# First chunk as two plain units, aligned accumulators, and a third pair of seven products in an fp32 encoder layer

## The chip, the cores and the metric

The kernel runs on one core of a Trainium2 chip. The metric is device time in microseconds (us) of one execution. The kernel before takes 2221.93 us (median of 3 runs, 2221.05 to 2222.04).

## What is computed

One encoder layer on 256 tokens of width 2048, in fp32. The change touches the two feed-forward halves:

```python
h = h + 0.5 * swiglu(rmsnorm(h, ffn1_norm[i]), ffn1_w_gate[i], ffn1_w_up[i], ffn1_w_down[i])
...  # mixer: neighbourhood attention, latent attention, gates, w_out
h = h + 0.5 * swiglu(rmsnorm(h, ffn2_norm[i]), ffn2_w_gate[i], ffn2_w_up[i], ffn2_w_down[i])
...  # per-layer embedding, final norm

def swiglu(x, w_gate, w_up, w_down):
    return (jax.nn.silu(x @ w_gate) * (x @ w_up)) @ w_down
```

The hidden width is 5632, that is 11 chunks of 512 columns; the inner width 2048 is 16 K tiles of 128.

## The kernel before

**Three matmuls for one.** Every operand is split into a rounded part hi and a rest lo (`split`, L89: ScalarE casts hi, VectorE subtracts to get lo). A product is then `triple` (L93): lo of x times hi of w, hi times hi, hi times lo, each a matmul of 128 columns of x against 128x512 of w.

**Joint blocks.** A `Block` (L170) computes gate and up of one chunk together, over 8 pairs of K tiles. Two token halves, two K tiles and two outputs make eight products per pair; a *plain pair* (`Plain`) does these eight, 24 matmuls. A *product pair* does seven products of sums (21 matmuls): its granule A (`SevenA`) holds three weights and forms sums of weights in place (L238, L240, L241 on VectorE), its granule B (`SevenB`) holds the four sums. `SEVEN` (L22) names the pairs that do so: 3 and 5. I write P0, P1, P2, A3, B3, P4, A5, B5, P6, P7 for a block's ten granules. The sums of x that go with them are the *forms*, made once per feed-forward half (`new_forms`, for the first pair `first_form`) and kept in X0 to X7.

**Accumulators.** The seven sums q1 to q7 of a block have fixed banks of PSUM (L192): q1 in bank 0, q6 in 1, q7 in 2, q3 in 3, q2, q4, q5 in 4 to 6; bank 7 is for transposes. A block's `early` evacuates q1, q6, q7, its `late` gives `first` (q2, q4) and `rest` (q5, q3, sigmoid, product). The result is transposed in two steps T0 and T1 (four small transposes each into bank 7, read by L310 on ScalarE and L311 on VectorE).

**Down.** After 4, 4 and 3 chunks (`PARTS`) four *units* of the down product follow. A unit takes two accumulators from banks 0 to 3 in turn (`acc_bank`, a counter that runs through the whole kernel). The mixer has one unit with a single accumulator, so the counter stands at an odd place when the second feed-forward half begins.

**What sets the order.** A list of granules, `grans`, is worked off at the end of the program: each step emits the matmuls of its granule, then the small tasks due at that step (`tasks`, filled by `at`). `convert` loads and splits granules ahead; a granule takes two of the six buffers W0 to W5 (an ordinary unit's granule one of W0 to W3), which come free when an earlier granule's matmuls are done. So at most three granules are split ahead. Raw weights come through three buffers R0 to R2 by DMAs from SP's queue. Each engine executes its own instructions in the order in which the program emits them. The last granule of a block, P7, calls `more[0]` (first), `convert`, `more[1]` (rest):

```python
        if ends:
            more[0]()
            convert()
            more[1]()
        free.extend(e.tags)
        for fn in tasks.pop(g, []):
            fn()
```

Of the kernel before, what the change touches and what calls it, by code (L numbers as in the profile page):

```python
# [14 lines left out]
P = 128  # L15
# [5 lines left out]
PARTS = ((0, 4), (4, 8), (8, 11))  # L21
SEVEN = {3, 5}  # L22
MLA_SCALE = 192 ** -0.5
# [4 lines left out]
def encoder_kernel(ctx, tc, x, p, ffn1_norm, ffn1_w_gate, ffn1_w_up, ffn1_w_down, mix_norm, w_in,  # L28
# [28 lines left out]

    seven_on = [True]
    spare = [7, 0, 1, 2]
    turn = {"acc": 0, "side": 0, "raw": 0}  # L60
# [4 lines left out]
    def bank():  # L65
        if seven_on[0]:
            turn["side"] += 1
            return psum_tile(spare[turn["side"] % len(spare)])
        turn["side"] += 1
        return psum_tile(4 + turn["side"] % 4)  # L70
# [29 lines left out]
    class Unit:  # L100
        def __init__(self, src, K, N, xop, evac, by_token=False, wide=False):
            self.src, self.K, self.N, self.xop, self.evac, self.by_token = src, K, N, xop, evac, by_token
            self.per = 4 if wide else 1024 // N
            self.load = 4 if wide else (2 * self.per if N == 512 else self.per)
            self.raw = self.ps = None
            self.kept = []
            for k0 in range(0, K, self.per):
                grans.append(Granule(self, k0, min(self.per, K - k0), wide))

    class Granule:  # L110
# [7 lines left out]
        def conv(self):  # L118
            u, k0, nk = self.u, self.k0, self.nk
            if k0 % u.load == 0:  # L120
                n = min(u.load, u.K - k0)
                u.raw = raw_piece([P, n, u.N])
# [47 lines left out]
    class Block:  # L170
        def __init__(self, srcs, form, early, late):
            self.srcs, self.form, self.early, self.late = srcs, form, early, late
            self.first = not grans
            self.q = {}
# [33 lines left out]
    class Plain(Pair):  # L208
        def conv(self):
            raw = first_raw(self) or raw_piece([P, 4, 512])  # L210
            self.blk.load(self.i, raw)
            self.hilo(4)
            if self.blk.first and self.i == 0:
                between = first_form()
                split(self.hi[:, 0:2, :], self.lo[:, 0:2, :], raw[:, 0:2, :])
                between()
                split(self.hi[:, 2:4, :], self.lo[:, 2:4, :], raw[:, 2:4, :])
                return
            split(self.hi, self.lo, raw)
# [11 lines left out]
    class SevenA(Pair):  # L231
        def conv(self):
            raw = first_raw(self) or raw_piece([P, 4, 512])
            raws[id(self.blk), self.i] = raw
# [8 lines left out]
        def matmuls(self):  # L243
            b, hi, lo = self.blk, self.hi, self.lo
            seven_on[0] = True
            f = b.form(self.i)
            for n, w, x in ((1, 0, 0), (2, 1, 1), (3, 2, 5)):
                b.add(n, f(x), hi[:, w, :], lo[:, w, :], n == 1 and self.i == max(SEVEN))

    class SevenB(Pair):  # L250
# [14 lines left out]
    def first_raw(p):  # L265
        return piece(f"H{p.i}", [P, 4, 512]) if p.blk.first and p.i < 4 else None

# [68 lines left out]
    forms = {}  # L336

    def new_forms(n, gname, js=(0, 1)):
        for j in js:
            i = 2 * n + j  # L340
            ps = bank()
            for k in range(2):
                for t in range(2):
                    PE.transpose(ps[:, k * T + t * P:k * T + t * P + P],
                                 h[:, t, (2 * i + k) * P:(2 * i + k + 1) * P], ident)
            z = piece("Z", [P, 8, P])
            gc = gcol[gname] + 2 * i
# [3 lines left out]
            S.activation(o1, p4[:, 0], AF.Copy, scale=gT[:, gc:gc + 1])
            S.activation(z[:, 2:4, :], p4[:, 1], AF.Copy, scale=gT[:, gc + 1:gc + 2])

            def minus(o, a, b):
                V.tensor_tensor(out=z[:, o, :], in0=z[:, a, :], in1=z[:, b, :], op=ALU.subtract)
            if seven:
                minus(4, 0, 3)
                minus(7, 1, 0)
                minus(5, 4, 1)
                V.tensor_tensor(out=z[:, 6, :], in0=z[:, 2, :], in1=z[:, 5, :], op=ALU.add)  # L360
                r, m = z[:, 1:8, :], 7
            else:
                V.tensor_tensor(out=z[:, 4:6, :], in0=z[:, 0:3:2, :], in1=z[:, 1:4:2, :], op=ALU.subtract)
                r, m = z[:, 0:6, :], 6
            f = piece(f"X{i}", [P, 2, m, P], F32R)
            split(f[:, 0], f[:, 1], r)
            forms[i] = f

    def first_form():
        ps = bank()  # L370
        for k in range(2):
            for t in range(2):
                PE.transpose(ps[:, k * T + t * P:k * T + t * P + P], h[:, t, k * P:(k + 1) * P], ident)
        f = piece("X0", [P, 2, 6, P], F32R)
        forms[0] = f
        p4 = ps.rearrange("p (k t c) -> p k t c", k=2, t=2)
        for k in range(2):
            S.activation(f[:, 0, 2 * k:2 * k + 2], p4[:, k], AF.Copy, scale=gT[:, k:k + 1])
        for k in range(2):
            V.scalar_tensor_tensor(out=f[:, 1, 2 * k:2 * k + 2], in0=p4[:, k], scalar=gT[:, k:k + 1],  # L380
                                   in1=f[:, 0, 2 * k:2 * k + 2].bitcast(F32), op0=ALU.mult, op1=ALU.subtract)

        def rest():
            z = piece("Z", [P, 8, P])
            for k in range(2):
                S.activation(z[:, 2 * k:2 * k + 2, :], p4[:, k], AF.Copy, scale=gT[:, k:k + 1])
            V.tensor_tensor(out=z[:, 4:6, :], in0=z[:, 0:3:2, :], in1=z[:, 1:4:2, :], op=ALU.subtract)
            split(f[:, 0, 4:6], f[:, 1, 4:6], z[:, 4:6, :])
        return rest

# [69 lines left out]
    def ffn(phase, wg, wu, wd, nxt):  # L460
# [43 lines left out]
        def down_evac(n, final):  # L504
# [545 lines left out]
    step[0] = -1  # L1050
    for a, b in ((256, 512), (512, 1024), (1024, 2048)):
        convert()
        nc.sync.dma_start(h[:, :, a:b], xr[:, :, a:b])
        if a == 256:
            new_forms(0, "ffn1", (1,))

    def begin(i):
        return lambda: new_forms(i // 2, "ffn1", (i % 2,))

# [6 lines left out]
    for i in range(2, 8):  # L1066
        tasks.setdefault((0, 1, 2, 2, 3, 4)[i - 2], []).append(begin(i))
    for n in range(4):
        tasks.setdefault(5 + n, []).append(late_stat(n))
    tasks.setdefault(30, []).append(lambda: gains(16, 72))  # L1070

    for g, e in enumerate(grans):
        step[0] = g
        if g == 3:
            del spare[1:]
        ends = isinstance(e, Pair) and e.end and not isinstance(e, SevenB)
        if g > 2 and not ends:
            convert()
        seven_on[0] = isinstance(e, Pair)
        more = e.matmuls()  # L1080
        if ends:
            more[0]()
            convert()
            more[1]()
        free.extend(e.tags)
        for fn in tasks.pop(g, []):
            fn()
        if g <= 2:
            convert()
    assert not tasks, sorted(tasks)  # L1090

# [38 lines left out]
```

## Time and profile before

| | |
|---|---|
| median of three runs | 2221.93 us |
| the profiled execution | 2220.76 us, of which span 2219.0 us |
| PE (TensorE) busy | 2186.1 us, 99% of the span |
| VectorE busy | 1471.8 us, 66% |
| ScalarE busy | 1030.8 us, 46% |
| mean granted TensorE clock | 0.993 |

TensorE works nearly all the time, so time goes in three ways only: matmuls that are issued, matmuls at the lower clock, and the few stretches in which TensorE waits. The shares of VectorE and ScalarE are means over stages; in the joint blocks they are higher.

### The profile page before, as it was taken

To read this page: it belongs to the slowest core of one execution; us is meant where nothing else is said; L and a number is where in the kernel's file an instruction comes from. 1 tells how busy PE (TensorE), PEld (TensorE's weight loads), DVE (VectorE), ACT (ScalarE), POOL (GpSimd) and SP (SyncE) were. 2 spreads that over 40 slices of the span, in tenths; PEclk is the share of its full clock that TensorE was granted. 3 is DMA by queue.
4 is the path that set the end of the run, shared out by engine and by line. 5 is a ranking of instruction groups with operands and counts; after the bars stand their busy time and mean duration, and the time that the engine had idled before them with its cause. 6 is when DMAs were issued, how large, how long until landed. Compare 5 with 4: busy or idle time off the path is not lost. (4 is left out here: it accounts for less than half of the span.)

```text
span 2219.0 us, 24699 instructions
## 1 busy us (share of the span) xinstructions
PE 2186.1 (99%) x9832; PEld 1801.9 (81%) x9832; DVE 1471.8 (66%) x1486; ACT 1030.8 (46%) x1042; POOL 35.8 (2%) x39
## 2 busy tenths in 40 slices
PE   8999999999999999999999999999999999999997
PEld 6788888888888887788888888887888878887886
DVE  6887468865786565555655556888558875687665
ACT  5544344543444454445544445545334543444453
POOL 0000000000000000040000000000000000000000
PEclk8999999999999999999999999999999999999999
DMA  5655555566556554475455555556555655566553
GB/s 193 218 190 198 194 195 179 190 215 198 175 192 207 162 183 139 135 213 182 146 192 191 191 184 199 171 188 212 188 171 195 213 192 191 180 204 210 178 174 126
DMA packets 211795, 413.54 MB, mean 186 GB/s; under 512 B 11704, under 2 KB 12288, under 8 KB 211552
## 3 DMA queue, kind: packets, MB, share of 16 engines
q1 hardware_dynamic: 210432, 408.46, 55.3%
q0 software_dynamic: 1216, 3.50, 0.7%
q8 instruction: 77, 1.26, 0.2%
q14 instruction: 38, 0.31, 0.0%
q10 hardware_dynamic: 32, 0.01, 0.0%
HBM read 409.83 MB, written 2.10 MB: 186 GB/s over the span
## 5 line engine op out<-in xcount | busy, mean ns | idle before, releaser
L91 DVE TENSOR_TENSOR W<-R,W 128x1024 fp32r<-128x1024 f32 (+2 forms) x587 | 965.7, 1660 | 500.3 <-ACT W L90 489.8
L90 ACT CAST W<-R 128x1024 fp32r<-128x1024 f32 (+2 forms) x587 | 816.2, 1402 | 796.2 <-PE B L96 367.4
L95 PE MATMUL B<-W,X 128*128 128x512 f32 x2132 | 842.8, 395 | 2.8 <-ACT W L90 1.5
L97 PE MATMUL B<-W,X 128*128 128x512 f32 x2132 | 833.1, 391 | 2.5 <-DVE W L91 2.4
L96 PE MATMUL B<-W,X 128*128 128x512 f32 x2132 | 832.1, 390 | 0.0
L97 PEld LDWEIGHTS B<-W,X 128*128 128x128 f32 x2132 | 401.3, 188 | 88.9 <-DVE W L91 4.2
L95 PEld LDWEIGHTS B<-W,X 128*128 128x128 f32 x2132 | 401.7, 188 | 87.8 <-issue 2.5
L96 PEld LDWEIGHTS B<-W,X 128*128 128x128 f32 x2132 | 401.7, 188 | 81.2
L95 PE MATMUL B<-W,H 128*128 128x512 f32 x832 | 327.4, 393 | 7.9 <-DVE pt L486 7.9
L97 PE MATMUL B<-W,H 128*128 128x512 f32 x832 | 325.3, 391 | 0.0
L96 PE MATMUL B<-W,H 128*128 128x512 f32 x832 | 325.2, 391 | 0.0
L95 PEld LDWEIGHTS B<-W,H 128*128 128x128 f32 x832 | 157.0, 189 | 41.1 <-ACT W L90 5.5
L97 PEld LDWEIGHTS B<-W,H 128*128 128x128 f32 x832 | 157.0, 189 | 33.0
L96 PEld LDWEIGHTS B<-W,H 128*128 128x128 f32 x832 | 157.1, 189 | 31.8
L310 ACT CAST H<-B 128x512 fp32r<-128x512 f32 x52 | 30.1, 587 | 183.3 <-PE B L327 183.3
L311 DVE TENSOR_TENSOR H<-B,H 128x512 fp32r<-128x512 f32 x52 | 35.6, 690 | 73.4 <-ACT H L310 73.4
L238 DVE TENSOR_TENSOR R<-R 128x1024 f32<-128x1024 f32 x43 | 52.7, 1225 | 1.5
L508 DVE SCALAR_TENSOR_TENSOR h<-B,h 128x512 f32<-128x512 f32 x48 | 32.9, 691 | 23.7 <-PE B L97 23.7
L315 ACT ACTIVATE X<-B,gT 128x256 fp32r<-128x256 f32 x40 | 15.7, 475 | 35.4 <-PE B L327 35.4
L240 DVE TENSOR_TENSOR R<-R 128x512 f32<-128x512 f32 x43 | 29.8, 692 | 1.5
L241 DVE TENSOR_TENSOR R<-R 128x512 f32<-128x512 f32 x43 | 29.8, 692 | 1.5
L327 PE MATMUL B<-ident,t 128*128 128x128 f32 x136 | 27.8, 272 | 0.0
(215 smaller groups left out, 942.4 us busy)
## 6 DMA issues: line engine op xcount, KB each, us to landing
R<-in_ffn_w_down_dram SPq DMA_DIRECT2D x88, 1024.0 KB, 5.1
R<-in_ffn_w_gate_dram SPq DMA_DIRECT2D x172, 512.0 KB, 3.7
R<-in_ffn_w_up_dram SPq DMA_DIRECT2D x172, 512.0 KB, 4.7
R<-in_w_in_dram SPq DMA_DIRECT2D x64, 1024.0 KB, 5.2
R<-in_w_out_dram SPq DMA_DIRECT2D x16, 1024.0 KB, 5.1
R<-in_w_pl_gate_dram SPq DMA_DIRECT2D x16, 1024.0 KB, 5.1
R<-in_w_branch_a_dram SPq DMA_DIRECT2D x8, 1024.0 KB, 5.1
R<-in_w_branch_b_dram SPq DMA_DIRECT2D x8, 1024.0 KB, 5.0
```

The source lines that it names most:

```text
L90: S.copy(hi, r)
L91: V.tensor_tensor(out=lo, in0=r, in1=hi.bitcast(F32), op=ALU.subtract)
L95: PE.matmul(o, xl, hi, start=start, stop=False)
L96: PE.matmul(o, xh, hi, start=False, stop=False)
L97: PE.matmul(o, xh, lo, start=False, stop=stop)
L238: V.tensor_tensor(out=raw[:, 0:4:3, :], in0=raw[:, 0:3:2, :], in1=raw[:, 3:4, :].to_broadcast([P, 2, 512]), op=ALU.add)
L240: V.tensor_tensor(out=raw[:, 2, :], in0=raw[:, 0, :], in1=raw[:, 2, :], op=ALU.add)
L241: V.tensor_tensor(out=raw[:, 1, :], in0=raw[:, 2, :], in1=raw[:, 1, :], op=ALU.add)
L310: S.copy(hi, ps.rearrange("p (k t) -> p k t", k=2))
L311: V.tensor_tensor(out=lo, in0=ps.rearrange("p (k t) -> p k t", k=2), in1=hi.bitcast(F32), op=ALU.subtract)
L327: PE.transpose(ps[:, k * T + t * P:k * T + t * P + P], srcs[t][:, (2 * j + k) * P:(2 * j + k + 1) * P], ident)
L508: V.scalar_tensor_tensor(out=hs, in0=ps[t], scalar=0.5, in1=hs, op0=ALU.mult, op1=ALU.add)
```

## The change

Four things change. (1) The first chunk of the first half is no joint block but two ordinary units, gate and then up, of 16 K tiles each, in granules of two K tiles; its forms of sums are made later (`more_forms`), while the up unit runs, and x is loaded in smaller pieces. (2) The accumulator counter is set to 0 at the first down unit of each part (`align`). (3) The product pairs are 2, 4 and 6, so a block is P0, P1, A2, B2, P3, A4, B4, P5, A6, B6, P7. (4) Since B6 stands right before P7, the tasks due at P7 (`early`) are emitted ahead of `first`.

```diff
-SEVEN = {3, 5}
+SEVEN = {2, 4, 6}
...
     class Unit:
-        def __init__(self, src, K, N, xop, evac, by_token=False, wide=False):
+        def __init__(self, src, K, N, xop, evac, by_token=False, wide=False, align=False):
+            self.align = align
...
+            self.early = not grans
+            if self.early:
+                self.load = 2
...
             if k0 == 0:
+                if u.align:
+                    turn["acc"] = 0
                 u.ps = [acc_bank() for _ in range(2 if u.N == 512 else 1)]
...
+    def first_forms(i):
+        p2 = plain_tiles(i)
...
+        for k in range(2):
+            S.activation(hi[k], p2[:, k], AF.Copy, scale=gT[:, 2 * i + k:2 * i + k + 1])
         for k in range(2):
+            V.scalar_tensor_tensor(out=lo[k], in0=p2[:, k], scalar=gT[:, 2 * i + k:2 * i + k + 1],
+                                   in1=hi[k].bitcast(F32), op0=ALU.mult, op1=ALU.subtract)
+
+        def keep():
+            z = zs[i // 4][:, i % 4].rearrange("p (k a) b -> p k (a b)", k=2)
             for k in range(2):
+                S.activation(z[:, k], p2[:, k], AF.Copy, scale=gT[:, 2 * i + k:2 * i + k + 1])
+        return keep
+
+    def more_forms(i):
+        e = tmp.tile([P, 4, P], F32, tag="s", name=nm("e"))
+        m = sums(zs[i // 4][:, i % 4], e, i)
+        split(forms[i][:, 0, 4:4 + m], forms[i][:, 1, 4:4 + m], e[:, 0:m, :])
...
+        def gate_evac(ps):
...
+        def up_evac(ps):
+            r = rstd[phase]
+            a = hold.pop("a")
+            for t in range(2):
+                V.scalar_tensor_tensor(out=a[t], in0=ps[t], scalar=r[:, t:t + 1], in1=a[t],
+                                       op0=ALU.mult, op1=ALU.mult)
...
+            at(1, tr(0))
+            at(2, tr(1))
+
         for c0, c1 in PARTS:
             for c in range(c0, c1):
-                block(c)
+                if grans:
+                    block(c)
+                else:
+                    unit(rows(wg, 0), 16, 512, first_xop, gate_evac)
+                    unit(rows(wu, 0), 16, 512, first_xop, up_evac)
...
                 unit(rows(wd[c0 * 512:c1 * 512], n * 512), 4 * (c1 - c0), 512, hop,
-                     down_evac(n, c1 == NC_FF), wide=True)
+                     down_evac(n, c1 == NC_FF), wide=True, align=(n == 0))
...
     for i in range(2, 8):
-        tasks.setdefault((0, 1, 2, 2, 3, 4)[i - 2], []).append(begin(i))
+        tasks.setdefault(i - 2, []).append(lambda i=i: first_forms(i)())
     for n in range(4):
-        tasks.setdefault(5 + n, []).append(late_stat(n))
-    tasks.setdefault(30, []).append(lambda: gains(16, 72))
+        tasks.setdefault(3 + n, []).append(late_stat(n))
+    for i in range(8):
+        tasks.setdefault(8 + i, []).append(lambda i=i: more_forms(i))
+    tasks.setdefault(7, []).append(lambda: gains(16, 72))
...
         if ends:
+            for fn in tasks.pop(g, []):
+                fn()
             more[0]()
```

VectorE's order where the up unit of the first chunk ends and the first joint block begins, in the changed kernel (W_81 is lo of P0's weights, W_86 of P1's, W_91 of A2's; e is a sum of x, X a form; B_67 and B_68 are the up unit's accumulators):

```order
L89 TENSOR_TENSOR W_81_520<-R_79_516,W_80_519 128x2048
L340 TENSOR_TENSOR e_535<-H_23_246 128x128 x2
...
L89 TENSOR_TENSOR X_27_275<-e_554,X_27_275 128x256
L89 TENSOR_TENSOR W_86_562<-R_84_558,W_85_561 128x2048
L340 TENSOR_TENSOR e_577<-H_23_246 128x128 x2
L340 TENSOR_TENSOR e_577<-e_577,H_23_246 128x128
L347 TENSOR_TENSOR e_577<-H_23_246,e_577 128x128
L89 TENSOR_TENSOR X_35_309<-e_577,X_35_309 128x512
L540 SCALAR_TENSOR_TENSOR t_417<-B_67_431,sm_388,t_417 128x512
L540 SCALAR_TENSOR_TENSOR t_418<-B_68_432,sm_388,t_418 128x512
```

The two L540 read the up unit's accumulators, banks 2 and 3. They stand behind the splits of P0 and P1 and the forms of pairs 4, 5 and 6.

VectorE's order between two joint blocks of a part, before (from the last evacuation of the old block: L91 are splits of P2 and A3, L238 to L241 the sums of weights, L311 reads T0):

```order
L490 SCALAR_TENSOR_TENSOR t_2222<-t_2222,sm_502,s_2253 128x512
L91 TENSOR_TENSOR W_329_2276<-R_327_2272,W_328_2275 128x2048
L91 TENSOR_TENSOR W_336_2311<-R_334_2307,W_335_2310 128x1536
L238 TENSOR_TENSOR R_334_2307<-R_334_2307 128x2x512
L240 TENSOR_TENSOR R_334_2307<-R_334_2307 128x512
L241 TENSOR_TENSOR R_334_2307<-R_334_2307 128x512
L311 TENSOR_TENSOR H_337_2341<-B_338_2342,H_337_2341 128x512
```

and in the changed kernel (the same place; L502 is L490, L240 to L243 are L238 to L241, L310 is L311):

```order
L502 SCALAR_TENSOR_TENSOR t_1194<-t_1194,sm_388,s_1192 128x512
L89 TENSOR_TENSOR W_183_1222<-R_181_1218,W_182_1221 128x1536
L240 TENSOR_TENSOR R_181_1218<-R_181_1218 128x2x512
L242 TENSOR_TENSOR R_181_1218<-R_181_1218 128x512
L243 TENSOR_TENSOR R_181_1218<-R_181_1218 128x512
L89 TENSOR_TENSOR W_189_1257<-R_181_1218,W_188_1256 128x2x512
L89 TENSOR_TENSOR W_189_1257<-R_181_1218,W_188_1256 128x1024
L310 TENSOR_TENSOR H_190_1286<-B_191_1287,H_190_1286 128x512
```

The split of P2 is gone from in front of the read of T0, and both splits of B2 now stand there.

TensorE's order at that place in the changed kernel (the last transpose of T0, the nine matmuls of A2, the first transpose of T1):

```order
L326 MATMUL B_339_2399<-ident,t_2306 128x128
L93 MATMUL B_343_2413<-W_330_2333,X_16_189 128x512
L94 MATMUL B_343_2413<-W_330_2333,X_16_189 128x512
L95 MATMUL B_343_2413<-W_331_2334,X_16_189 128x512
L93 MATMUL B_332_2340<-W_330_2333,X_16_189 128x512
L94 MATMUL B_332_2340<-W_330_2333,X_16_189 128x512
L95 MATMUL B_332_2340<-W_331_2334,X_16_189 128x512
L93 MATMUL B_335_2361<-W_330_2333,X_16_189 128x512
L94 MATMUL B_335_2361<-W_330_2333,X_16_189 128x512
L95 MATMUL B_335_2361<-W_331_2334,X_16_189 128x512
L326 MATMUL B_344_2423<-ident,pt_2307 128x128
```

In the kernel before the 24 matmuls of P2 stand between T0 and T1.

## Rows read from the trace of the kernel before

**Rows 1.** What TensorE waited for: us in total, times, longest us

```profile
PE B L95 <- DVE pt L486: 7.9, 3, 3.2
```

**Rows 2.** Timeline of TensorE: start us, us, engine, line, operation, [idle before <-releaser]

```profile
59.44 0.39 PE L95 MATMUL B<-W,X 128*128 128x512 f32 x1
...
68.28 0.45 PE L95 MATMUL B<-W,X 128*128 128x512 f32 x1
...
80.46 0.27 PE L327 MATMUL B<-ident,pt 128*128 128x128 f32 x1
```

**Rows 3.** A steady joint block: us, busy of PE, PEld, DVE, ACT, POOL

```profile
107.69:150.85 43.16, 43.16 (x196) 35.71 (x195) 35.42 (x32) 21.21 (x17) 0.00 (x0) 1.00 0.58 196
```

**Rows 4.** Groups by line and shape: busy us, mean ns | idle before

```profile
L90 ACT CAST W<-R 128x2048 fp32r<-128x2048 f32 x217 | 415.0, 1912 | 366.1 <-PE B L96 274.4 <-DMA R<-in_ffn_w_up_dram 35.7 <-DVE W L91 32.2
L90 ACT CAST W<-R 128x1024 fp32r<-128x1024 f32 x327 | 340.9, 1053 | 358.9 <-PE B L97 237.4 <-DVE R L238 86.1 <-PE B L96 22.4
...
L91 DVE TENSOR_TENSOR W<-R,W 128x2048 fp32r<-128x2048 f32 x217 | 494.9, 2290 | 265.5 <-ACT W L90 256.1 <-PE B L96 9.3
L91 DVE TENSOR_TENSOR W<-R,W 128x1024 fp32r<-128x1024 f32 x327 | 398.5, 1229 | 223.1 <-ACT W L90 222.0
L91 DVE TENSOR_TENSOR W<-R,W 128x1536 fp32r<-128x1536 f32 x43 | 75.3, 1752 | 11.7 <-ACT W L90 11.7
L238 DVE TENSOR_TENSOR R<-R 128x1024 f32<-128x1024 f32 x43 | 52.7, 1225 | 1.5
...
L240 DVE TENSOR_TENSOR R<-R 128x512 f32<-128x512 f32 x43 | 29.8, 692 | 1.5
```

**Rows 5.** Timeline of VectorE, steady block: start of `early`, last of `rest`

```profile
107.69 0.68 DVE L470 TENSOR_TENSOR pt<-B,t 128x512 f32<-128x512 f32 x1
...
110.18 0.69 DVE L479 TENSOR_TENSOR pt<-B,t 128x512 f32<-128x512 f32 x1 [0.48 <-PE B L97]
...
117.20 0.75 DVE L490 SCALAR_TENSOR_TENSOR t<-t,sm,s 128x512 f32<-128x512 f32 x1
```

**Rows 6.** Timeline of TensorE, first down units of the second half

```profile
1553.63 0.47 PE L95 MATMUL B<-W,H 128*128 128x512 f32 x1 [2.35 <-DVE pt L486]
...
1557.29 0.46 PE L95 MATMUL B<-W,H 128*128 128x512 f32 x1
...
2037.27 0.47 PE L95 MATMUL B<-W,H 128*128 128x512 f32 x1 [3.17 <-DVE pt L486]
...
2038.73 0.63 PE L95 MATMUL B<-W,H 128*128 128x512 f32 x1
...
2042.13 0.40 PE L97 MATMUL B<-W,H 128*128 128x512 f32 x1
```

**Rows 7.** Timeline of TensorE, first chunk

```profile
35.97 1.12 PE L344 MATMUL B<-ident,h 128*128 128x128 f32 x4 [3.00 <-ACT Z L352]
```

**Rows 8.** Timeline of ScalarE, first chunk: x, weights, squares

```profile
5.80 0.84 ACT L378 ACTIVATE X<-B,gT 128x256 fp32r<-128x256 f32 x2 [3.51 <-PE B L373]
...
16.11 1.91 ACT L90 CAST W<-H 128x2048 fp32r<-128x2048 f32 x1 [1.30 <-DMA H<-in_ffn_w_up_dram]
...
52.22 0.62 ACT L401 ACTIVATE sq<-h 128x512 f32<-128x512 f32 x1
...
53.46 1.89 ACT L90 CAST W<-R 128x2048 fp32r<-128x2048 f32 x1
```

**Rows 9.** Timeline of VectorE, first chunk: sums of x, then the statistics

```profile
27.36 0.69 DVE L355 TENSOR_TENSOR Z<-Z 128x128 f32<-128x128 f32 x3
...
32.71 0.42 DVE L363 TENSOR_TENSOR Z<-Z 128x256 f32<-128x256 f32 x1
...
63.66 0.15 DVE L444 TENSOR_REDUCE sm<-sm 128x2 f32<-128x8 f32 x1
...
66.02 0.16 DVE L423 SCALAR_TENSOR_TENSOR sm<-sm,sm 128x2 f32<-128x2 f32 x1
```

**Rows 10.** Timeline of TensorE, first joint block of the second half

```profile
1400.94 0.50 PE L97 MATMUL B<-W,X 128*128 128x512 f32 x1 [0.33 <-DVE W L91]
```

More of the change, by code (lines that the diff above doesn't have):

```diff
@@ L56, in slot @@
         return piece(SLOT[i], shape, dt)
-    seven_on = [True]
-    spare = [7, 0, 1, 2]
+    seven_on = [False]
     turn = {"acc": 0, "side": 0, "raw": 0}
@@ L66, in bank @@
         if seven_on[0]:
-            turn["side"] += 1
-            return psum_tile(spare[turn["side"] % len(spare)])
+            return psum_tile(7)
         turn["side"] += 1
@@ L121, in conv @@
                 n = min(u.load, u.K - k0)
-                u.raw = raw_piece([P, n, u.N])
+                if u.early and k0 < 12:
+                    if k0 % 4 == 0:
+                        u.space = piece(f"H{k0 // 4}", [P, 4, u.N])
+                    u.raw = u.space[:, k0 % 4:k0 % 4 + 2, :]
+                else:
+                    u.raw = raw_piece([P, n, u.N])
                 nc.sync.dma_start(u.raw, u.src(k0, n))
@@ L172, in __init__ @@
             self.srcs, self.form, self.early, self.late = srcs, form, early, late
-            self.first = not grans
             self.q = {}
@@ L209, in conv @@
         def conv(self):
-            raw = first_raw(self) or raw_piece([P, 4, 512])
+            raw = raw_piece([P, 4, 512])
             self.blk.load(self.i, raw)
             self.hilo(4)
[L213 to L218, printed above, removed]
             split(self.hi, self.lo, raw)
@@ L263, in matmuls @@
                 at(1, lambda: b.early(b.q))
-    def first_raw(p):
-        return piece(f"H{p.i}", [P, 4, 512]) if p.blk.first and p.i < 4 else None
     def rows(w, c0, N=512):
@@ L336, in encoder_kernel, with sums, minus, plain_tiles @@
     forms = {}
+    def sums(a, o, i):
+        def minus(out, x, y):
+            V.tensor_tensor(out=out, in0=x, in1=y, op=ALU.subtract)
+        if i not in SEVEN:
+            minus(o[:, 0:2, :], a[:, 0:3:2, :], a[:, 1:4:2, :])
+            return 2
+        minus(o[:, 0, :], a[:, 1, :], a[:, 3, :])
+        minus(o[:, 3, :], a[:, 0, :], a[:, 1, :])
+        minus(o[:, 1, :], o[:, 0, :], a[:, 0, :])
+        V.tensor_tensor(out=o[:, 2, :], in0=a[:, 2, :], in1=o[:, 1, :], op=ALU.add)
+        return 4
+    def plain_tiles(i):
+        ps = bank()
+        for k in range(2):
+            for t in range(2):
+                PE.transpose(ps[:, k * T + t * P:k * T + t * P + P],
+                             h[:, t, (2 * i + k) * P:(2 * i + k + 1) * P], ident)
+        return ps.rearrange("p (k a) -> p k a", k=2)
     def new_forms(n, gname, js=(0, 1)):
@@ L351, in new_forms @@
[L351 to L364, printed above, removed]
+            for k in range(2):
+                S.activation(z[:, 2 * k:2 * k + 2, :].rearrange("p a b -> p (a b)"), p2[:, k], AF.Copy,
+                             scale=gT[:, gc + k:gc + k + 1])
@@ L365, in new_forms @@
+            m = 4 + sums(z[:, 0:4, :], z[:, 4:8, :], i)
             f = piece(f"X{i}", [P, 2, m, P], F32R)
-            split(f[:, 0], f[:, 1], r)
+            split(f[:, 0], f[:, 1], z[:, 0:m, :])
             forms[i] = f
-    def first_form():
-        ps = bank()
-        for k in range(2):
[L372 to L376, printed above, removed]
-        for k in range(2):
[L378 to L384, printed above, removed]
-            for k in range(2):
[L386 to L389, printed above, removed]
@@ new lines, in encoder_kernel @@
+    zs = {}
+    def first_forms(i):
+        p2 = plain_tiles(i)
+        if i % 4 == 0:
+            zs[i // 4] = piece(("Z", "H3")[i // 4], [P, 4, 4, P])
+        f = piece(f"X{i}", [P, 2, 8 if i in SEVEN else 6, P], F32R)
+        forms[i] = f
+        hi, lo = [[f[:, b, 2 * k:2 * k + 2, :].rearrange("p a b -> p (a b)") for k in range(2)] for b in range(2)]
+        for k in range(2):
+            S.activation(hi[k], p2[:, k], AF.Copy, scale=gT[:, 2 * i + k:2 * i + k + 1])
+        for k in range(2):
+            V.scalar_tensor_tensor(out=lo[k], in0=p2[:, k], scalar=gT[:, 2 * i + k:2 * i + k + 1],
+                                   in1=hi[k].bitcast(F32), op0=ALU.mult, op1=ALU.subtract)
+        def keep():
+            z = zs[i // 4][:, i % 4].rearrange("p (k a) b -> p k (a b)", k=2)
+            for k in range(2):
+                S.activation(z[:, k], p2[:, k], AF.Copy, scale=gT[:, 2 * i + k:2 * i + k + 1])
+        return keep
@@ L391, in form, with first_xop @@
+    def more_forms(i):
+        e = tmp.tile([P, 4, P], F32, tag="s", name=nm("e"))
+        m = sums(zs[i // 4][:, i % 4], e, i)
+        split(forms[i][:, 0, 4:4 + m], forms[i][:, 1, 4:4 + m], e[:, 0:m, :])
+    def first_xop(kt):
+        f = forms[kt // 2]
+        k = kt % 2
+        return tuple(f[:, b, 2 * k:2 * k + 2, :].rearrange("p a b -> p (a b)") for b in range(2))
     def form(i):
@@ L511, in down_evac, with tr, f @@
             return f
+        hold = {}
+        def gate_evac(ps):
+            r = rstd[phase]
+            hold["a"] = tmps("t")
+            for t in range(2):
+                s = tmp.tile([P, 512], F32, tag="s", name=nm("s"))
+                S.activation(s, ps[t], AF.Sigmoid, scale=r[:, t:t + 1])
+                V.scalar_tensor_tensor(out=hold["a"][t], in0=ps[t], scalar=r[:, t:t + 1], in1=s,
+                                       op0=ALU.mult, op1=ALU.mult)
+        def up_evac(ps):
+            r = rstd[phase]
+            a = hold.pop("a")
+            for t in range(2):
+                V.scalar_tensor_tensor(out=a[t], in0=ps[t], scalar=r[:, t:t + 1], in1=a[t],
+                                       op0=ALU.mult, op1=ALU.mult)
+            def tr(j):
+                def f():
+                    if j == 0:
+                        hT[0] = piece("H0", [P, 2, 4, T], F32R)
+                    transpose_chunk(a, hT[0], js=(j,))
+                return f
+            at(1, tr(0))
+            at(2, tr(1))
         for c0, c1 in PARTS:
             for c in range(c0, c1):
-                block(c)
+                if grans:
+                    block(c)
+                else:
+                    unit(rows(wg, 0), 16, 512, first_xop, gate_evac)
+                    unit(rows(wu, 0), 16, 512, first_xop, up_evac)
             down = len(grans)
@@ L1050, in encoder_kernel @@
     step[0] = -1
-    for a, b in ((256, 512), (512, 1024), (1024, 2048)):
+    keep = [first_forms(0)]
+    for _ in range(14):
+        PE.transpose(idle[:, 0:P], ident, ident)
+    for a, b in ((256, 512), (512, 1024), (1024, 1536)):
         convert()
@@ L1084, in encoder_kernel @@
             more[1]()
-        free.extend(e.tags)
         for fn in tasks.pop(g, []):
             fn()
-        if g <= 2:
+        if g <= 5:
             convert()
+        free.extend(e.tags)
     assert not tasks, sorted(tasks)
```

25 lines of the change are left out of this document (8 added, 17 removed).

## Prediction

> **What bounds the kernel now.** I read the waits of TensorE first: it is busy 99% of the span, and of the little that it waits, the largest piece is three waits of 7.9 us together for L486, the last read of a block's accumulators [rows 1]. The timeline shows that they stand before the first down unit of each part of the second half, and nowhere in the first half [rows 6]: in the second half the accumulator counter is odd, so the first unit wants bank 3, which `rest` frees last. Everywhere else TensorE goes from matmul to matmul. So I looked next at what one matmul costs. In the timeline 39 of them lie between 59.44 and 68.28 us [rows 2], 0.2267 us each; a plain granule of 24 takes 5.44 us, A 2.04, B 2.72. Then I asked how much room VectorE has, since a product pair buys three matmuls of TensorE with sums on VectorE: in a steady block of 43.16 us it is busy 35.42 [rows 3]. Last I went through the first chunk engine by engine, because the change rewrites it.
>
> The profiled execution took 2220.76 us, 1.2 under the median of the three runs. The sum is made against it.
>
> **Fewer matmuls.** A joint block falls from 186 to 183 matmuls, 0.68 us. There are 21 joint blocks in the changed kernel. The first of them I count with the start; the other 20 give -13.6 us if TensorE stays the bound.
>
> **Room on VectorE.** A plain split costs 2.25 us there (2.29 with its overlap). A product pair costs 1.75 + 1.23 + 0.69 + 0.69 for A and its sums and 2 x 1.23 for B, 6.82 in all [rows 4]. One more pair makes 35.42 + 6.82 - 2.25 = 40.0 us of work in a block of 42.5. It fits with 2.5 us to spare, if its waits fit too. I followed one block by the durations of [rows 4, 5], counted from the end of the old P7. P7's and P0's splits hang on the end of P5 (buffer free, cast 1.9, split 2.25, split 2.25), which is 10.2 before the end of P7, so P0's split ends at -3.75. `early` and `first` take 2.7, to -1.05; P1's split 2.2, to 1.1; `rest` 4.9, to 6.0. A2 with its sums ends at 10.45, B2 at 12.9, and L310's VectorE partner, the read of T0, at 13.55. TensorE does P0, P1, T0, A2 by 5.44 + 5.44 + 0.5 + 2.04 = 13.4 and then wants bank 7 for T1: it waits 0.2. Before, all of P2 lay between T0 and T1, 5.4 us of cover; the order list shows that this cover shrinks to the nine matmuls of A2, with both splits of B2 put ahead of the read. Behind T1, P3, P5 and P7 are split 0.8 us before they are due, A and B 0.5 to 4 us. So the new wait is 0.2 us (bounds 0 and 1, since it is a difference of two long sums) at each of the 15 places where a joint block follows another in the same part (7 in the first half, 8 in the second): +3 us, range 0 to +15.
>
> **Down units.** With the counter at 0 the first unit takes banks 0 and 1 (q1, q6). `early` reads them by about -2.4 us in the ledger above, though it now runs behind P0's split (or that of the first down granule). So the three waits go: -7.9 [rows 1]. After the first wait nine matmuls start 3.66 us apart in sum (1553.63 to 1557.29) where 2.04 would do, and after the third eight take 3.40 (2038.73 to 2042.13) where 1.81 would: TensorE had stood idle and ran 0.43 us per matmul, the lower of its two clocks (1.2 against 2.4 GHz) [rows 6]. That goes too, -3.2. Together -11.1; next in line is only the second unit, two to three granules later, on banks 2 and 3. Bounds -11.1 and 0.
>
> **First block of the second half.** There VectorE also makes the forms of pairs 6 and 7 and the statistics. Before, P4 was split at 1400.9, 0.33 us late [rows 10]. Now the fifth granule is P3, due 5.44 us earlier. VectorE has one plain split less ahead of it (2.25), but pair 6's sums are four small operations and not one, and its split is longer, about +0.9. If VectorE was never idle there, P3 is 0.3 + 5.44 - 2.25 + 0.9 = 4.4 late; if it was idle by as much as the difference, 0.3. I take 2.6, which the durations give when I lay them out from the transposes on, so +2.3.
>
> **Start.** The gate unit has ScalarE as its bound: per granule two casts of x, two kept copies (0.84 each pair), one cast of weights (1.0), 2.7 us against 2.72 of matmuls and 0.5 of transposes; four pairs of squares at 1.24 (52.22 to 53.46) come on top [rows 4, 8]. From 5.80: 8 x 2.7 + 5.0 + 2.0 for the first two up granules = 34.4; 0.6 for the second transposes and 1.5 for the fourth weights (before, the same number of bytes had landed at 16.11 [rows 8]) make 36.5. The statistics take 2.4 on VectorE [rows 9], to 39.0; two sigmoids, priced like two squares, the gate's evacuation (two of 0.75) and the split of up granule 3 end at 43.0. Then four rounds of a sum of x (0.42, or 0.95 for a product pair), its cast (0.45 to 0.6), the weights' cast (1.0) and split (1.23), each waiting for the one before, VectorE and ScalarE in turn: 3.1 + 3.1 + 3.9 + 3.1, to 56.2. P0's cast and split end at 59.2. TensorE can have done 18 of P0's 24 matmuls at 62.8. The next wants bank 3, and that is an accumulator of the up unit. Its evacuation stands, in VectorE's order, behind the forms of pair 4 (2.4), of 5 (0.9 to the cast), P1's cast and split (1.9 + 2.3), the forms of 6 (2.4), and takes 1.5: 59.2 + 11.4 = 70.6. **TensorE waits 7.8 us**, a wait that the kernel before does not have. Then six matmuls, T0 and P1 end at 77.9 at full clock; the two waits of [rows 6] that were followed by the lower clock cost 1.6 each, the one of 3.00 at 35.97 [rows 7] more, so I add 2.0: 79.9. Before, the same stage (P0, P1, one T) is reached at 80.46 + 0.5 = 80.95 [rows 2]. With the block's own 0.68 the start gives -1.7. It would have given about -9.5 without that wait; the old start's waits and slow stretches are paid back. Bounds -9.5 and +4 (ScalarE 3 us later, clock down for longer).
>
> The Trainium skill, TensorE: Matmul & The Clock Gate, Part 1, says that the throttled state is the default and activity releases it. By that rule the 7.8 us wait hands back the full clock; the rows at 1553.63 and 2038.73 agree, and without the rule the start would give 2.0 more. The same page (first table) says that VectorE's queue is strictly first in, first out; if it were not, the two reads of the up accumulators could pass the forms and the 7.8 us would go. No row of this trace shows one instruction passing another.
>
> **Sum.** -1.7 - 13.6 + 3.0 - 11.1 + 2.3 = -21.1: 2220.8 - 21.1 = 2199.7 for an execution like the profiled one, about 2201 as a median.
>
> **Rivals.**
> 1. *The wait in P0 is not there or short* (the statistics end sooner, or the casts overlap better than I let them): 7.8 us less, 2193. For it: the ledger chains 40 durations. Against: the order is fixed, and the forms alone are 5.7 us ahead of the read.
> 2. *T1 waits about 1 us*: 15 x 0.8 more, 2213. For it: the read of T0 has no margin. Against: VectorE's part of the ledger is made of durations that hardly vary [rows 4].
> 3. *The alignment gains nothing* (another wait is as late as L486): 2212. For it: `early` moves behind P7. Against: the first half has had these banks at its down units, and no wait there.
> 4. *VectorE becomes the bound of the joint blocks.* It was idle 43.16 - 35.42 = 7.7 us per block [rows 3], in waits for casts and freed buffers [rows 4]. Only 2.5 may remain. If more does, every block is longer by the excess; if 4.6 remain, 44.6 us, +1.4 against before over 20 blocks: -1.7 + 29 - 11.1 + 2.3 = +18, 2240. From 3.7 on there is no gain left. For it: 94% occupancy with handovers to ScalarE. Against: the ledger keeps 0.5 to 1 us of margin at each plain granule.
>
> **Chances.** My forecast 0.53 (2195 to 2207), rival 1 0.16, rival 2 0.14, rival 3 0.06, rival 4 0.11. Range: 2190 to 2214 takes in the first four and leaves out rival 4 and the tails. A measurement of this kernel can tell about 0.2% (4.4 us) from no change: faster 0.86 (all but rival 4 and some of the tails of 2 and 3), same 0.05, slower 0.09 (most of rival 4).
>
> **What would show it.** A wait of 6 to 9 us of TensorE at 63 to 71 us, ended by L540; no wait for L498 (the old L486) at the down units, and full clock there; joint blocks of 42.5 to 42.9 us with VectorE busy about 40; small waits of the transposes for L310; one wait of 2 to 3 us in the second half's first joint block, ended by a split. I am wrong if a steady block takes 43.2 or more, if TensorE waits for splits (L89) in every block, or if the first joint block's P1 ends before 74 or after 85 us.

## The result, and the profile after

The changed kernel takes 2200.32 us (median of 4 runs, 2200.09 to 2202.47), the kernel before 2221.49 beside it: ratio 0.9908, interval 0.9892 to 0.9923. The forecast was 2201, range 2190 to 2214. The profiled execution took 2200.09 us with a span of 2198.2, 20.8 less span than before. (Line numbers have moved: L486 of before is L498 now, L90 and L91 are L88 and L89, L311 and L327 are L310 and L326.)

What TensorE waited for, changed kernel (us in total, times, longest us):

```profile
PE B L93 <- DVE t L540: 6.9, 1, 6.9
PE B L95 <- DVE W L89: 4.4, 5, 2.4
PE B L93 <- DVE X L384: 4.0, 3, 2.1
...
PE B L354 <- ACT Z L365: 0.9, 1, 0.9
```

The waits of [rows 1] are gone: there is none for L498. In their place stands the forecast wait for L540 in the first chunk (6.9 us; forecast 7.8), and one of 2.4 for a split in the second half's first joint block, where [rows 10] had 0.33:

```profile
1394.37 0.50 PE L95 MATMUL B<-W,X 128*128 128x512 f32 x1 [2.43 <-DVE W L89]
```

None is for L310: the transposes T1, forecast to wait 0.2 us at 15 places, wait nowhere.

Two steady joint blocks (us, then busy time and count of PE, PEld, DVE, ACT, POOL; granted clock), the answer to [rows 3]:

```profile
111.74:154.19 42.45, 42.45 (x193) 35.14 (x192) 39.56 (x38) 23.00 (x20) 0.00 (x0) 1.00 0.59 199
154.19:196.63 42.44, 42.44 (x193) 35.13 (x192) 39.55 (x38) 22.98 (x20) 0.00 (x0) 1.00 0.58 197
```

TensorE does not wait in them, and VectorE has 2.9 us to spare. How near it is to the edge stands where T1 begins. VectorE's read of T0, then the first and last transpose of T1 on TensorE (timelines):

```profile
128.07 0.68 DVE L310 TENSOR_TENSOR H<-B,H 128x512 fp32r<-128x512 f32 x1
```

```profile
128.97 0.27 PE L326 MATMUL B<-ident,pt 128*128 128x128 f32 x1
...
129.30 0.27 PE L326 MATMUL B<-ident,t 128*128 128x128 f32 x1
```

The read ends at 128.75 (128.07 and 0.68), 0.2 us before the transposes that need its bank.

The first chunk on ScalarE: its kept copies (L390: x, scaled, put into memory for the forms of sums that are made later), each behind VectorE's pass over the same accumulator (L384).

```profile
19.08 0.84 ACT L390 ACTIVATE Z<-B,gT 128x256 f32<-128x256 f32 x2 [1.34 <-DVE X L384]
22.93 0.84 ACT L390 ACTIVATE H<-B,gT 128x256 f32<-128x256 f32 x2 [1.34 <-DVE X L384]
26.79 0.84 ACT L390 ACTIVATE H<-B,gT 128x256 f32<-128x256 f32 x2 [1.34 <-DVE X L384]
31.86 0.84 ACT L390 ACTIVATE H<-B,gT 128x256 f32<-128x256 f32 x2 [1.34 <-DVE X L384]
36.94 0.84 ACT L390 ACTIVATE H<-B,gT 128x256 f32<-128x256 f32 x2 [1.34 <-DVE X L384]
...
42.01 1.04 ACT L88 CAST W<-R 128x1024 fp32r<-128x1024 f32 x1
44.88 1.27 ACT L532 ACTIVATE s<-B,sm 128x512 f32<-128x512 f32 x2 [1.83 <-DVE sm L435]
```

The trace ends each of these waits by L384; in the program both lines only read the accumulator. The prediction's ledger let ScalarE run without those waits: last square done at 36.5 us, in the trace 42.0. What follows is 4 to 6 us late. Where TensorE then stops:

```profile
36.56 0.50 PE L93 MATMUL B<-W,X 128*128 128x512 f32 x1 [2.06 <-DVE X L384]
...
74.99 0.80 PE L93 MATMUL B<-W,X 128*128 128x512 f32 x1 [6.91 <-DVE t L540]
```

L540 is done at 74.9 (forecast 70.6), and T1 begins at 84.5 (forecast 79.9). The stretch around the wait, and the matmuls right behind it, with the granted clock third from the end:

```profile
60.00:80.00 20.00, 13.09 (x49) 9.91 (x48) 14.68 (x21) 7.58 (x8) 0.00 (x0) 0.83 0.47 157
75.00:79.50 4.50, 4.50 (x13) 3.62 (x14) 3.04 (x4) 2.37 (x3) 0.00 (x0) 0.50 0.16 62
```

The matmuls behind the wait ran at the lower of the two clocks, to 79.4 us.

**The sum against the forecast.** Each block's transposes T0 and T1 (L327 before, L326 after) are marks that both traces have. How far apart two marks lie, after less before, gives what a stage lost or gained:

```
term                                       forecast   trace
start, with the first joint block             -1.7     +2.7
20 further joint blocks, 0.68 each           -13.6    -13.6
T1 waiting for the read of T0                 +3.0      0
three first down units of the second half    -11.1    -12.0
first joint block of the second half          +2.3     +2.0
the rest                                       0       +0.1
sum                                          -21.1    -20.8
```

The start, for one: the fourth chunk's last transposes begin at 217.25 us against 215.94, +1.3, though two steady blocks ahead of them gave 1.36; so +2.7. The first row is the kernel before:

```profile
215.94 0.27 PE L327 MATMUL B<-ident,pt 128*128 128x128 f32 x1
```

```profile
217.25 0.27 PE L326 MATMUL B<-ident,pt 128*128 128x128 f32 x1
```

Seven blocks of the first half behind that mark take 4.77 us less, 0.68 each. That the total came out right is in part luck: two errors, +4.4 and -3.0, nearly cancel.

### The profile page after: what moved, and what is told of

Its sections match the earlier page's. It is cut to its first block, busy times and chain, and to the rows that moved or that the text cites. A ratio compares the mean times of both kernels' runs of the same rounds, so it can differ in the third digit from the quotient of the medians.

```text
span 2198.2 us, 24815 instructions
## 1 busy us (share of the span) xinstructions
PE 2168.6 (99%) x9789; PEld 1787.7 (81%) x9789; DVE 1550.7 (71%) x1601; ACT 1068.0 (49%) x1100; POOL 35.8 (2%) x39
## 5 line engine op out<-in xcount | busy, mean ns | idle before, releaser
L89 DVE TENSOR_TENSOR W<-R,W 128x1024 fp32r<-128x1024 f32 (+2 forms) x633 | 1008.1, 1604 | 460.6 <-ACT W L88 459.1
L88 ACT CAST W<-R 128x1024 fp32r<-128x1024 f32 (+2 forms) x633 | 855.7, 1358 | 858.7 <-DVE R L240 275.0
L93 PE MATMUL B<-W,X 128*128 128x512 f32 x2113 | 834.1, 395 | 11.3 <-DVE t L540 6.9
L95 PE MATMUL B<-W,X 128*128 128x512 f32 x2113 | 824.6, 390 | 4.4 <-DVE W L89 4.4
L94 PE MATMUL B<-W,X 128*128 128x512 f32 x2113 | 823.4, 390 | 0.0
L93 PEld LDWEIGHTS B<-W,X 128*128 128x128 f32 x2113 | 397.2, 188 | 95.9 <-DVE t L540 7.3
L95 PEld LDWEIGHTS B<-W,X 128*128 128x128 f32 x2113 | 397.0, 188 | 90.7 <-DVE W L89 7.2
L94 PEld LDWEIGHTS B<-W,X 128*128 128x128 f32 x2113 | 397.4, 188 | 80.1
L240 DVE TENSOR_TENSOR R<-R 128x1024 f32<-128x1024 f32 x63 | 77.2, 1225 | 2.2
L310 DVE TENSOR_TENSOR H<-B,H 128x512 fp32r<-128x512 f32 x52 | 35.3, 686 | 25.1 <-ACT H L309 25.1
L242 DVE TENSOR_TENSOR R<-R 128x512 f32<-128x512 f32 x63 | 43.6, 692 | 2.2
L243 DVE TENSOR_TENSOR R<-R 128x512 f32<-128x512 f32 x63 | 43.6, 692 | 2.1
L326 PE MATMUL B<-ident,t 128*128 128x128 f32 x140 | 28.4, 276 | 0.0
```

Source lines behind the costliest of these rows:

```text
L88: S.copy(hi, r)
L89: V.tensor_tensor(out=lo, in0=r, in1=hi.bitcast(F32), op=ALU.subtract)
L93: PE.matmul(o, xl, hi, start=start, stop=False)
L94: PE.matmul(o, xh, hi, start=False, stop=False)
L95: PE.matmul(o, xh, lo, start=False, stop=stop)
L240: V.tensor_tensor(out=raw[:, 0:4:3, :], in0=raw[:, 0:3:2, :], in1=raw[:, 3:4, :].to_broadcast([P, 2, 512]), op=ALU.add)
```

## The experiments

Times are medians; the kernel before, run beside them, took 2220.8 to 2221.4 us. All but one of these kernels start from the changed one.

**No restart of the count.**

```
-                     down_evac(n, c1 == NC_FF), wide=True, align=(n == 0))
+                     down_evac(n, c1 == NC_FF), wide=True)
```

> The changed kernel without the restart of the accumulator count. My theory: the eight down units of the second half wait for the evacuation again, 7.9 us in seven waits of 3.0 and less, and the clock falls behind two of them (3.2 us): 11.1 us more than the changed kernel, 2211 us, with waits for L498 of 2 to 3 us near 1530 and 2015 us. Rival (rival 3 of the forecast): the waits come back but their time is made good elsewhere, or they do not come back because the new start has shifted the count: 2200 us.

Measured: 2217.4 us (ratio to before 0.9986, interval 0.9977 to 0.9995; 10 runs from 2214.3 to 2219.9). The restart is worth 17.1 us here, not 11. The waits are three, one at each part, as in [rows 1]; the expectation's "seven" is a slip. Waits of TensorE, then the place of the first:

```profile
PE B L93 <- DVE pt L498: 8.9, 3, 3.0
```

```profile
1551.86 0.77 PE L93 MATMUL B<-W,H 128*128 128x512 f32 x1 [2.96 <-DVE pt L498]
1552.42 0.63 PE L94 MATMUL B<-W,H 128*128 128x512 f32 x1
...
1557.11 0.63 PE L93 MATMUL B<-W,H 128*128 128x512 f32 x1
...
1557.97 0.42 PE L95 MATMUL B<-W,H 128*128 128x512 f32 x1
1558.23 0.39 PE L93 MATMUL B<-W,H 128*128 128x512 f32 x1
```

From 1551.86 to 1557.97 fourteen matmuls start 6.1 us apart in sum, where 3.2 would do: the lower clock costs 2.9 us. It did so again behind the second wait (2.95 us, at 1814.79), and for a shorter stretch behind the third (2.95, at 2035.24). In the kernel before the same three waits were 2.35, 2.35 and 3.17, and the second was not followed by the lower clock. Between the two traces lie 18.5 us: 17.1 at the three first down units, and 1.4 at 1394 us, where this kernel lost the full clock and the changed one did not (last section). So the mechanism is the forecast one, and its price depends on what else is there. The spread over the runs goes with the clock: the mean granted clock is 0.992 in the five slowest runs (2217.7 to 2219.9) and 0.993 to 0.995 in the five fastest (2214.3 to 2217.1).

**The restart alone, in the kernel before.**

```
...
+                if u.align:
+                    turn["acc"] = 0
...
-                     down_evac(n, c1 == NC_FF), wide=True)
+                     down_evac(n, c1 == NC_FF), wide=True, align=(n == 0))
```

> The kernel before with the restart of the accumulator count alone. My theory: the seven waits for L486 (7.9 us) and the lower clock behind them (3.2 us) go, nothing else moves: 2210 us. Rival: half of it comes back as other waits in the down units, 2216 us.

Measured: 2209.0 us (0.9947, 0.9932 to 0.9961). No wait for L486 is left, and nothing came in its place. The three stages at the marks shrink by 4.2, 2.6 and 5.0 us, 11.9 together: 7.9 of waits, and 1.9, 0.3 and 1.9 behind them. The 0.3 stands at the wait that kept the full clock. A row counts a wait from the end of a matmul of 0.39 us, while matmuls start 0.227 apart, so the loss is 0.16 more than the row says, and the first matmul behind a wait takes 0.31 instead of 0.227 to the next (1817.40 to 1817.71, last section). The forecast of 11.1 lacked these 0.3 us at each of the three waits; the 3.2 that it had for the clock is what is left. Rival 3 is out.

**Two pairs instead of three.**

```
-SEVEN = {2, 4, 6}
+SEVEN = {3, 5}
```

> The changed kernel with two of the eight pairs of a joint block as seven products instead of three, that is {3, 5}. My theory: each of the 20 steady blocks goes from 42.45 us back to 43.16 us, +14.2 us, and the 2.1 us that the second half's first block lost to a split go away: +12 us, 2212 us. Rival: the blocks were partly bound by VectorE in both kernels, then a block gets back less than 0.7 us and the kernel lies at 2205 us or below.

Measured: 2211.1 us (0.9957, 0.9942 to 0.9972), 10.8 more than with three pairs. At the marks the steady blocks are back to 43.13 us, as in the kernel before, the long split wait of the second half is gone (longest 0.5), and the start's wait for L540 is shorter, since of the pairs 4, 5 and 6, whose forms stand ahead of it, one makes four sums now and not two of them:

```profile
PE B L93 <- DVE t L540: 5.6, 1, 5.6
PE B L93 <- DVE X L384: 4.0, 3, 2.1
PE B L95 <- DVE W L89: 2.4, 5, 0.5
```

So the third pair saves 0.68 us in each of the 21 joint blocks, 14.3, and at the marks pays 3.6 of it back at two places where VectorE is already late: 1.6 in the first chunk, 2.0 in the second half's first block.

**The start alone** (two pairs and no restart).

```
-SEVEN = {2, 4, 6}
+SEVEN = {3, 5}
...
-                     down_evac(n, c1 == NC_FF), wide=True, align=(n == 0))
+                     down_evac(n, c1 == NC_FF), wide=True)
```

> The first chunk as two plain units alone: no restart of the count, two pairs as seven products. My theory: the start costs 2.9 us less 0.7 us or so of products, and saves nothing, since ScalarE's kept copies wait for VectorE's pass over the same accumulator: 2 to 4 us slower than the kernel before, 2224 us. Rival (the forecast's own step for the start): 1.0 to 1.7 us faster than the kernel before, 2220 us.

Measured: 2220.7 us against 2220.8, ratio 1.0002, interval 0.9992 to 1.0011: the start alone is worth nothing that can be told. In the trace it costs 2.0 us at the fourth chunk's transposes; the trace gets them back at the last part, where the wait for L498 is shorter than before and the lower clock does not follow it (the three waits are 7.1 together, longest 2.4). I had expected 2224, so the price at the mark was right and the median lower; the forecast's gain of 1 to 1.7 us is not in the trace either.

**Four pairs.**

```
-SEVEN = {2, 4, 6}
+SEVEN = {1, 2, 4, 6}
```

> The changed kernel with four pairs as seven products, {1, 2, 4, 6}. VectorE's 39.55 us a block grow by the difference that one pair made (39.55 less 35.42 is 4.1 us) to 43.7 us, TensorE's 42.45 us shrink by 0.7 to 41.7 us. My theory: VectorE bounds the block, 43.7 us or more, so each of 20 blocks loses at least 1.2 us against 42.45: 2225 to 2240 us, with waits of TensorE for splits (L89) and for T0 or T1 in each block. Rival: TensorE's products still bound, 0.7 us a block less: 2186 us.

Measured: 2292.0 us (1.0327, 1.0303 to 1.0351), far more than the 2225 to 2240 expected. A steady block, and the waits of TensorE:

```profile
131.40:177.70 46.30, 42.10 (x182) 34.42 (x182) 42.15 (x41) 24.89 (x21) 0.00 (x0) 0.96 0.53 177
```

```profile
PE B L326 <- DVE H L310: 38.5, 15, 2.7
PE B L93 <- DVE pt L497: 23.2, 15, 1.8
```

In 46.3 us TensorE is idle for 4.2 and VectorE for 4.15: neither is full. VectorE has less work than expected (42.15, not 43.7), and the block is longer all the same. TensorE waits for the read of T0, 2.7 us, and again for `rest`, 1.5; VectorE waits in its turn for casts. This is rival 4 of the prediction, one pair further on: about 4 us of VectorE's idle time cannot be filled. With three pairs 2.9 remain and no wait appears. How much of the loss is the number of pairs and how much that pair 1 stands where T0 and T1 are was not separated.

**Kept copy ahead of the low part.** VectorE subtracts from the copy in memory instead of reading the accumulator.

```
+        z = zs[i // 4][:, i % 4].rearrange("p (k a) b -> p k (a b)", k=2)
         for k in range(2):
-            V.scalar_tensor_tensor(out=lo[k], in0=p2[:, k], scalar=gT[:, 2 * i + k:2 * i + k + 1],
-                                   in1=hi[k].bitcast(F32), op0=ALU.mult, op1=ALU.subtract)
...
+            S.activation(z[:, k], p2[:, k], AF.Copy, scale=gT[:, 2 * i + k:2 * i + k + 1])
+        for k in range(2):
+            V.tensor_tensor(out=lo[k], in0=z[:, k], in1=hi[k].bitcast(F32), op=ALU.subtract)
+        return lambda: None
```

> The changed kernel with ScalarE's kept copy of the scaled transposes made ahead of VectorE's low part, which is then the kept copy less the high part (read from memory instead of the accumulator). The result is the same. My theory: the first chunk came out 4.6 us longer than forecast because the kept copies (L390) wait for VectorE's pass (L384) over the same accumulator, six waits of 1.34 us and more; here ScalarE waits for nothing of VectorE, its last square ends 5 us earlier, near 37 us, L540 is done near 70 us instead of 74.9, and the kernel lies at 2195 to 2197 us. Rival: ScalarE waits for the transposes or VectorE's now longer chain all the same, the wait for L540 stays near 6.9 us: 2200 us.

Measured: 2194.9 us (0.9883, 0.9868 to 0.9898), 5.5 less than the changed kernel. ScalarE, the end of the squares, and TensorE at its wait:

```profile
31.27 0.89 ACT L385 ACTIVATE H<-B,gT 128x256 f32<-128x256 f32 x2
...
36.25 0.25 ACT L410 ACTIVATION_READ_ACCUMULATOR sq<-h 128x1 f32 x1
36.34 1.10 ACT L88 CAST W<-R 128x1024 fp32r<-128x1024 f32 x1
39.27 1.27 ACT L529 ACTIVATE s<-B,sm 128x512 f32<-128x512 f32 x2 [1.84 <-DVE sm L432]
```

```profile
69.39 0.79 PE L93 MATMUL B<-W,X 128*128 128x512 f32 x1 [6.92 <-DVE t L537]
```

The copies no longer wait for VectorE. The last square ends at 36.5, the statistics let the sigmoids go at 39.3, the evacuation is done at 69.3, T1 begins at 79.3. The prediction had 36.5, 39.0, 70.6 and 79.9: its ledger meets this kernel's times within 1.3 us, and at the fourth chunk's mark the start is worth -2.5, forecast -1.7. So the waits that it left out are what it had wrong there. Not every term is met: ScalarE's first step is at 6.87 instead of 5.80 and it still waits 2.8 us for transposes and weights where the ledger had 2.1, which its work, shorter than in the ledger, makes good. The edit also changes what VectorE reads, but its pass is only about 0.1 us shorter by that (0.76 to 0.79 for 0.87), eight times. Half of my expectation here was wrong: the wait for the evacuation did not shrink (6.92), because TensorE came 5.6 us earlier as well. What it saved were the waits for X (4.0 us) and their consequences.

**Sums one step ahead.**

```
+    ready = {}
+
+    def make_sums(i):
+        e = tmp.tile([P, 4, P], F32, tag="s", name=nm("e"))
+        ready[i] = e, sums(zs[i // 4][:, i % 4], e, i)
+
     def more_forms(i):
-        e = tmp.tile([P, 4, P], F32, tag="s", name=nm("e"))
-        m = sums(zs[i // 4][:, i % 4], e, i)
+        if i == 0:
+            make_sums(0)
+        e, m = ready.pop(i)
         split(forms[i][:, 0, 4:4 + m], forms[i][:, 1, 4:4 + m], e[:, 0:m, :])
+        if i < 7:
+            make_sums(i + 1)
```

> The changed kernel with the sums of each granule of the first joint block made one step ahead of its forms, so that ScalarE and VectorE do not take turns waiting for each other. My theory: of the chain that ends in L540 it is ScalarE's work and the alternation with VectorE that count, so L540 is done 3 to 5 us earlier and the kernel lies at 2196 to 2198 us. Rival: ScalarE is busy throughout that stretch and the order makes no difference: 2200 us.

Measured: 2193.7 us (0.9879, 0.9862 to 0.9895), 6.6 less, and more than the 2 to 4 that I expected. It is the same work in another order. VectorE in the changed kernel, one round of sum, cast (ScalarE) and split:

```profile
71.95 0.29 DVE L347 TENSOR_TENSOR e<-H,e 128x128 f32<-128x128 f32 x1
72.92 0.69 DVE L89 TENSOR_TENSOR X<-e,X 128x512 fp32r<-128x512 f32 x1 [0.68 <-ACT X L88]
73.53 1.40 DVE L540 SCALAR_TENSOR_TENSOR t<-B,sm,t 128x512 f32<-128x512 f32 x2
```

and with the sums ahead:

```profile
66.47 0.68 DVE L89 TENSOR_TENSOR X<-e,X 128x512 fp32r<-128x512 f32 x1
67.07 0.42 DVE L340 TENSOR_TENSOR e<-H 128x256 f32<-128x256 f32 x1
67.41 1.40 DVE L549 SCALAR_TENSOR_TENSOR t<-B,sm,t 128x512 f32<-128x512 f32 x2
```

From 55 us to the evacuation VectorE waits nine times in the changed kernel, 5.75 us in all, each time for a cast of ScalarE, which in its turn waits for VectorE's sum; here twice, 0.93. The wait for L540 falls from 6.9 to 1.4, and the granted clock of 60 to 80 us is 1.00, so the lower clock behind the wait is saved as well.

**Four granules' forms behind the evacuation.**

```
-        tasks.setdefault(8 + i, []).append(lambda i=i: more_forms(i))
+        tasks.setdefault((8, 9, 10, 11, 17, 19, 21, 22)[i], []).append(lambda i=i: more_forms(i))
```

> The changed kernel with the last four K granules of the first gate unit's forms made behind the first chunk's evacuation instead of ahead of it. My theory: what sets the wait of 6.9 us for L540 is the queue of forms ahead of the evacuation on ScalarE and VectorE: with four of them behind, L540 is done 5 us or more earlier, the wait and the lower clock after it shrink below 2 us, and some of it returns as waits for splits or forms in the next pair: 2193 to 2197 us. Rival: the same time is lost again behind the evacuation, since the first joint block needs the forms: 2200 us or more.

Measured: 2199.2 us (0.9900, 0.9885 to 0.9915), 1.2 less than the changed kernel: between my theory and the rival, and nearer to the rival. The wait for L540 is gone and T1 begins at 75.9 instead of 84.5, 8.6 us earlier; by the fourth chunk's transposes 2.0 are left. TensorE in the first joint block:

```profile
82.33 0.50 PE L95 MATMUL B<-W,X 128*128 128x512 f32 x1 [0.60 <-DVE W L89]
93.53 0.50 PE L95 MATMUL B<-W,X 128*128 128x512 f32 x1 [0.66 <-DVE W L89]
102.71 0.50 PE L93 MATMUL B<-W,X 128*128 128x512 f32 x1 [1.86 <-ACT W L88]
103.97 0.50 PE L95 MATMUL B<-W,X 128*128 128x512 f32 x1 [0.52 <-DVE W L89]
```

The forms have only moved; so have the waits, and the lower clock with them (the granted clock of 104 to 110 us is 0.72).

**Both: kept copy first, and sums ahead.** The two edits above together.

> The changed kernel with both: the kept copy ahead of the low part, and the sums of the first joint block's granules one step ahead. Apart they took 5.5 and 6.6 us off. My theory: the first removes waits of TensorE for X of 4.0 us between 30 and 40 us (and ScalarE's for VectorE), the second the wait for L540, and the 1.4 us that are left of that wait go as well: 4.0 and 1.4 us less than with the sums alone, 2188 to 2189 us. Rival: both shortened the same chain up to L540, so together they give no more than the better one: 2193 to 2194 us.

Measured: 2185.9 us (0.9841, 0.9828 to 0.9855), 14.5 less than the changed kernel and 35.5 less than before. The two gains add (5.5 and 6.6), with some 2 us on top, and it is 2 us better than I expected. One part of the expectation failed: the wait of 1.4 us stays. Of the waits between the first weights (1.2 us there) and the first block's end only this is left:

```profile
62.15 0.50 PE L93 MATMUL B<-W,X 128*128 128x512 f32 x1 [1.43 <-DVE t L546]
```

At the fourth chunk's transposes this kernel is 13.6 us ahead of the kernel before, two steady blocks' 1.36 in it: its start is worth -12.2, where the changed kernel's was +2.7.

## Why the prediction came out right

*Fewer matmuls, and TensorE as the bound*: right in mechanism and size, 0.68 us a block (42.45 against 43.13), and shown by taking a pair away.

*Room on VectorE*: forecast 40.0 us of work in 42.5, measured 39.55. The ledger had the read of T0 end 0.2 us after T1 wants its bank; it ends 0.2 us before, so the term of +3.0 is nothing. That was a difference of two long sums, and rival 2 was that near. With one pair more those waits are there, 2.7 us each, and the block is longer by what VectorE cannot fill, as rival 4 has it: 42.15 us of work and 4.15 of idle time make 46.3.

*Down units*: right. The term was 0.9 too small: the clock's 3.2 was met, but each of the three waits cost 0.3 us more than its row, whatever the clock. Alone the restart is 12.4 us by the medians; with three pairs and no restart 17.1.

*First block of the second half*: 2.6 forecast, 2.43 measured (+2.0 at the marks); with two pairs it is not there.

*Start*: wrong by 4.4, and the sign with it. The step that failed: "per granule two casts of x, two kept copies (0.84 each pair), one cast of weights (1.0), 2.7 us". ScalarE is not free to take them in a row: its copy waits for VectorE's L384, which itself waits behind a split. With the copies freed, the times that followed from the step are met within 1.3 us. The wait for L540, its place in the program and its cause were right (6.9 for 7.8; the kernel before does wait there too, but only 0.9 us, at 72.15 for L485). It stands 4 to 5 us later than forecast; P1 ends at 84.5, just short of the 85 us that would have been a sign of being wrong. From the end of L540 to T1 the trace has 9.6 us, the forecast 9.3 with its 2.0 for the clock; the granted clock behind the wait is 0.50. The rule of the Trainium skill weighed there (TensorE: Matmul & The Clock Gate, Part 1: activity releases the throttle, and the default is throttled) agrees with that. Rival 1, 2193 us, was wrong for the changed kernel; with the sums made ahead its condition holds, a short wait (1.4), and the time is 2193.7.

The three parts are not independent. By medians, restart and third pair are worth 12.4 us (restart, in the kernel before), 3.3 (third pair, with the new start and no restart), 10.8 (third pair, with both), 9.6 (restart, with the new start and two pairs) and 17.1 (restart, with both). So most of what the third pair gives needs the restart; that is measured. Why the waits for L498 grow from 2.4 to 2.95 with it was not tested.

## What to carry to other kernels

In a ledger of two engines, look up for each step what it waits for, not only its duration: here two engines that only read the same accumulator ran one behind the other. Where two engines alternate on one chain, start the next round's first step before the last one of this round; it added no work here and gave 6.6 us. A gain that one engine pays for with another's time (three pairs) can end before that other engine is full: here VectorE's 39.6 us in a block of 42.4 cost nothing in a steady block, and the next pair, with 42.2 us, made the block 46.3 us and the kernel 92 us slower.

## What was not expected of the hardware

The lower clock after a stall is not a function of the stall's length alone. A wait of 2.35 us was followed by matmuls at the lower clock at 1553.63 us in the kernel before, and the same 2.35 a part later was not; TensorE in the kernel before:

```profile
1817.40 0.47 PE L95 MATMUL B<-W,H 128*128 128x512 f32 x1 [2.35 <-DVE pt L486]
1817.71 0.39 PE L96 MATMUL B<-W,H 128*128 128x512 f32 x1
1817.94 0.40 PE L97 MATMUL B<-W,H 128*128 128x512 f32 x1
```

The wait near 1394 us kept the full clock in the changed kernel and lost it without the restart, though the two traces agree up to there within 0.4 us (the granted clock is the third column from the end):

```profile
1380.00:1420.00 40.00, 37.07 (x164) 30.26 (x165) 34.38 (x45) 24.50 (x27) 0.00 (x0) 1.00 0.52 172
```

```profile
1380.00:1420.00 40.00, 36.96 (x157) 30.11 (x158) 32.99 (x44) 23.79 (x25) 0.00 (x0) 0.96 0.48 160
```

The first row is the changed kernel, the second the one without the restart. Four more kernels have this wait of 2.43 us. The granted clock of 1380 to 1420 us is 1.00 again with the sums ahead, and 0.96 again with the kept copy first, with the late forms and with both. What decides it, these traces do not show. So a price for such a stall is open by up to three microseconds, as the 5.6 us between the ten runs without the restart suggest.
